# First stage of a two-layer decoder trunk on one core: rotary tables, bias tables, bias rows and the high part of h moved, and unit 0 put ahead of the values

## The chip, the cores and the metric

The kernel runs on one core of a Trainium2 chip. The metric is the device time of one execution in microseconds, the median of the timed runs.

## The reference

Two layers (DEPTH 2) work on 256 tokens of width 1024 in float32. Each layer modulates its input, projects it to three groups of attention heads, maps their output back, normalises, and does the same around an MLP. Only the first layer's beginning is touched by the change:

```python
mod = jax.nn.silu(c) @ ada_w[l] + ada_b[l]
sh_a, sc_a, g_a, sh_m, sc_m, g_m = [m_[:, None, :] for m_ in jnp.split(mod, 6, axis=-1)]
h = x * (1 + sc_a) + sh_a
parts = jnp.split(h @ w_in[l], SPLIT_POINTS, axis=-1)
...
ob, _ = banded_attention(rope(bq, positions), rope(bk, positions), bv, B_WINDOW - 1, sinks=sinks[l])
oc = nsa_attention(cq, ckc, cvc, cks, cvs, ckw, cvw, cg, cmp_pos[l], cmp_w1[l], cmp_w2[l], bias_c)
```

`rope` rotates the B heads by angles positions x frequencies; the A and C heads add a relative bias `rel_bias[t5_bucket(distance)]` to their scores.

## The kernel before, in words

**Split products.** A float32 product is made of three products of parts: `parts` (lines 174 to 183) writes the high part of a tile as fp32r with ScalarE (line 181, `whi`) and the low part with VectorE (line 182, `wlo`, the tile less its high part). `hT[:, 0]` and `hT[:, 1]` are the high and the low part of h, transposed.

**The first stage** (lines 898 to 938) goes over the 8 chunks of 128 columns of h, `kc`. For each chunk `first_h` (line 296) loads the chunk's modulation weights (1024 KB, line 139, `raw`) and, for every second chunk, x (line 302); multiplies the weights with silu(c) in 32 small matmuls (`gemv_mm`, line 169) into a PSUM bank `gv`; copies the result to `rs` (ScalarE, line 308); transposes x into columns 256 to 511 of the same bank (line 311); and brings scale and shift of the chunk into columns 128 and 129 of it (line 312). Then VectorE makes `md` (lines 314, 316) and `h32` (line 318), ScalarE the high part of hT (line 319) and VectorE the low part (line 320). `first_load` (line 323) loads the chunk's projection weights in two tiles `w0` (line 329; four buffers, so two chunks), and `first_chunk` (line 333) multiplies them with hT into seven open PSUM tiles (lines 341 to 344 for five pairs `prs`, lines 386 to 388 for two value tiles `vs`). An iteration of the loop traces gemv and loads of chunk kc, then the products of chunk kc-1, with the bank products and hT of chunk kc between them.

**Who sets the order.** The program is written tile by tile; when it is built, a scheduler lays the instructions of each engine into one queue, by the order in which they were traced and by when it estimates their inputs to be there, and puts in the semaphores. Each engine then works through its queue in that order. SyncE (SP) issues nearly all DMAs. `tc.issue_after(ins)` ties the instructions of its block that run on the engine of `ins` behind `ins` in that queue, and binds no other engine.

**START.** The string at place kc of `START` (line 34) says what else is traced after iteration kc: `r` loads a one-hot table and rel_bias, multiplies them (line 601, `bt`), copies the product (line 604) and sends it to DRAM through the POOL queue (`bias_rows`, line 592); each `b` loads a third of the `bias` table from there (`bias_tables`, line 612; 512 KB each); `p` loads `p2` (340 KB; sinks, compression positions and others), `c` loads `co` (373.5 KB; masks, rotary frequencies and others), and `o` makes the rotary tables `cosT` and `sinT` (`rope_tables`, line 621): a load of the positions, 14 VectorE instructions and two Sin on ScalarE, which need a table load. In the kernel before, `r` stands at chunk 0, `bpbco` at chunk 6 and a last `b` at chunk 7.

**After the stage** the open tiles are copied out (lines 995 to 1002, `vc_out` at line 948, whose Exp for the gates needs the Exp table), and the string `ORDER[0]` (line 32) is worked off: `k` projects and rotates the keys of the B heads (`bk_out`, line 970), `v` projects values (`vab_out`, line 965), `0` to `7` are the attention units of the C heads (`c_unit`, line 686: scores at line 697, `softmax_head` at lines 651 and 653), `s` is a step of the compression, and a dot is a step of the gemvs that fill in.

Of the kernel before, what the change touches and what calls it, by code (L numbers as in the profile page):

```python
# [13 lines left out]
AF = mybir.ActivationFunctionType  # L14
OP = mybir.AluOpType
# [13 lines left out]
EARLY = 3  # L29
FO = (1, 3)  # L30
TURN = 6
ORDER = ('kv0..21s4.3sa5.s.Acb.6.B7C..Ee', '.ts..q0412...ss3s.kva5cb.67AB.E..Ce')
GV = ('v', None, 'v', 'v', 'v')
START = ('r', '', '', '', '', '', 'bpbco', 'b', '')
GROUPS = ((0, 4, 0), (4, 8, 32))


# [84 lines left out]
def trunk_kernel(ctx: ExitStack, tc: tile.TileContext, a):  # L122
    nc = tc.nc
# [11 lines left out]
    p1 = cst.tile([128, NP1], F32, name="p1")  # L135
# [9 lines left out]
    co = cst.tile([128, NCO], F32, name="co")  # L145
# [3 lines left out]
    p2 = cst.tile([128, NP2], F32, name="p2")  # L149
# [7 lines left out]
    nc.vector.reciprocal(se[:, 1], se[:, 0])  # L157
    nc.vector.tensor_tensor(se[:, 2], cT, se[:, 1], op=OP.mult)
    silu = se[:, 2]
    crep = cst.tile([128, KC, 32], F32, name="crep")  # L160
    nc.vector.tensor_copy(crep, se[:, 2][:, :, None].to_broadcast([128, KC, 32]))

    hT = big.tile([128, 2, KC, S], F32R, name="hT")
# [132 lines left out]
    def first_h(kc):  # L296

        gv = ps.tile([128, 512], F32, name="gv", tag="pt")
        tp = gv[:, 256:512].rearrange("p (b t) -> p b t", b=2)
        t = rawload(a["ada0"][kc])  # L300
        if kc % 2 == 0:
            nc.sync.dma_start(x[:, :, kc * 128:kc * 128 + 256], a["x"][:, :, kc * 128:kc * 128 + 256])
        for k in range(KC):
            for s in range(2):
                j = 2 * (k % 2) + s
                end = gemv_mm(gv, t, k, j, (k * 2 + s) * 128, 128, k < 2, k >= KC - 2)
        rs = u2("rs")
        nc.scalar.activation(rs[:, :128], gv[:, :128], AF.Copy)
        yield end.ins
        for b in range(2):  # L310
            nc.tensor.transpose(tp[:, b], x[:, b, kc * 128:kc * 128 + 128], ident)
        nc.tensor.matmul(gv[:, 128:130], rs[:, :128], p1[:, 24:26], start=True, stop=True)
        md = sm.tile([128, 2], F32, name="md0")
        nc.vector.scalar_tensor_tensor(md[:, 0:1], gv[:, 128:129], 1.0, p1[:, 8 + 2 * kc:9 + 2 * kc],
                                       op0=OP.add, op1=OP.add)
        nc.vector.tensor_tensor(md[:, 1:2], gv[:, 129:130], p1[:, 9 + 2 * kc:10 + 2 * kc], op=OP.add)
        h32 = u2("h32")[:, :S]
        nc.vector.tensor_scalar(h32, gv[:, 256:512], md[:, 0:1], md[:, 1:2], op0=OP.mult, op1=OP.add)
        nc.scalar.activation(hT[:, 0, kc], h32, AF.Copy)
        nc.vector.tensor_tensor(hT[:, 1, kc], h32, hT[:, 0, kc].bitcast(F32), op=OP.subtract)  # L320
        yield

    def first_load(kc):
        off, _, n = CHUNK_OFF[0][f"k{kc}"]
        src = flat(a["w_in"][0], off, n)
        out = []
        for c, m in ((0, 768), (768, n - 768)):
            t = att.tile([128, 1024], F32, name="w0", tag="mx", bufs=4)
            nc.sync.dma_start(t[:, :m], src[:, c:c + m])
            out.append((t[:, :m], m))  # L330
        return out

    def first_chunk(kc, ts, prs, vs):

# [253 lines left out]
    bias = cst.tile([128, 12, 256], F32, name="bias")  # L588
    cosT = cst.tile([128, S], F32, name="cosT")
    sinT = cst.tile([128, S], F32, name="sinT")  # L590
# [30 lines left out]
    def rope_tables():  # L621
        pi32 = att.tile([128, S], I32, name="pi32", tag="pTc", bufs=2)
        src = a["positions"]
        nc.sync.dma_start(pi32, bass.AP(tensor=src.tensor, offset=src.offset, ap=[[0, 128], [1, S]]))
        t = new_P()
        an, k, f = t[:, 0], t[:, 1], t[:, 2]
# [17 lines left out]
        nc.vector.tensor_scalar(k, an, -1.0, -math.pi, op0=OP.mult, op1=OP.add)  # L644
        nc.vector.tensor_tensor(f, f, k, op=OP.max)
        nc.scalar.activation(sinT, f, AF.Sin)
        nc.vector.tensor_scalar(sinT, sinT, cc("sgn", 1), None, op0=OP.mult)


# [23 lines left out]
    def new_P():  # L673
        return att.tile([128, 4, S], F32, name="P", tag="P", bufs=4)
# [228 lines left out]
    btab = iter(())  # L903
    for kc in range(KC + 1):
        h = first_h(kc) if kc < KC else iter(())
        if kc == 0:
            next(h)
            w0 = first_load(0)
        if kc:
            ch = first_chunk(kc - 1, w0, prs, vs)  # L910
            end = next(h, None)
            if kc < KC:
                w0 = first_load(kc)
            for _ in range(FO[1]):
                next(ch)
            if FO[0] and end:
                with tc.issue_after(end):
                    next(ch)
            next(h, None)
            next(h, None)  # L920
            for _ in ch:
                pass
        else:
            next(h)
        for j in START[kc]:
            if j == "c":
                nc.sync.dma_start(co, a["co"])
            elif j == "r":
                btab = bias_tables(bias_rows())
            elif j == "p":  # L930
                nc.sync.dma_start(p2, a["p2"])
            elif j == "o":
                rope_tables()
            else:
                next(btab)
    for l in range(DEPTH):
        nc.vector.tensor_scalar(nsink[l], pp("sink", 4 * l, 4), -1.0, None, op0=OP.mult)
    fill += [gemv(0, 3, GV[0]), gemv(0, 2, GV[1])]
# [1 line left out]
    for l in range(DEPTH):  # L940
# [111 lines left out]
        jobs["+"] = lambda: next(btab)  # L1052
        for j in ORDER[l]:
            jobs[j]()
# [180 lines left out]
```

## Time and profile before

| | us |
|---|---|
| median of 3 runs | 701.38 (701.24 to 701.81) |
| the profiled execution | 700.93 |
| its span | 699.2 |

| engine | busy us | share of the span |
|---|---|---|
| TensorE (PE) | 672.6 | 96% |
| VectorE (DVE) | 490.3 | 70% |
| ScalarE (ACT) | 401.7 | 57% |
| GpSimd (POOL) | 41.0 | 6% |

The span runs from the first to the last instruction of the profiled execution; the rest of its time lies around it. An engine is idle when its next instruction waits; the profile names what ended such a wait. A matmul's duration overlaps the next one's, so the starts of a row of matmuls tell more than their durations.

### The profile page before, as it was taken

How to read it: one execution, taken by the hardware profiler on the slowest of the kernel's cores; microseconds unless marked ns; L12 is line 12 of the kernel's file. 1: busy time of each engine (PE TensorE's matmuls, PEld its weight loads, DVE VectorE, ACT ScalarE, POOL GpSimd, SP SyncE). 2: the span in 40 equal slices, each digit the busy share in tenths (PEclk: the TensorE clock that was granted, in tenths of full speed). 3: DMA queues.
4: the chain of work that ended last, by engine and by line, in shares of the span. 5: the costliest groups of instructions: out<-in, count | busy, mean ns of one | idle time of the engine just before them, and what ended most of it. 6: DMA issues, size and time to landing. Idle time of an engine off the chain costs nothing.

```text
span 699.2 us, 11153 instructions
## 1 busy us (share of the span) xinstructions
PE 672.6 (96%) x4284; PEld 549.5 (79%) x4284; DVE 490.3 (70%) x955; ACT 401.7 (57%) x791; POOL 41.0 (6%) x41
## 2 busy tenths in 40 slices
PE   5998899999999999999999999999999999999994
PEld 4898658458888888788889967867898888888883
DVE  3455865557798878888887866657679755555745
ACT  2346473776664656465746356688474655656641
POOL 0000100000400000000013020000130000000004
PEclk9999999999999999999999999999999999999998
DMA  8998586557369899899863858710448965555501
GB/s 323 354 356 329 211 331 213 187 218 321 137 229 373 296 389 322 322 345 340 302 240 121 328 187 281 266 60 2 181 129 305 372 214 193 208 183 182 181 0 61
DMA packets 29698, 167.68 MB, mean 240 GB/s; under 512 B 3215, under 2 KB 6827, under 8 KB 12108
## 3 DMA queue, kind: packets, MB, share of 16 engines
q1 hardware_dynamic: 29580, 166.94, 65.1%
q8 instruction: 34, 0.56, 0.3%
q14 instruction: 20, 0.16, 0.1%
q0 software_dynamic: 64, 0.02, 0.0%
HBM read 165.87 MB, written 1.08 MB: 239 GB/s over the span
## 4 chain that ended last, share of the span: by engine, by line
PE 88%; DVE 4%; ACT 3%; DMA 2%; issue 1%; SPq 0%; POOL 0%; POOLq 0%; DVEq 0%; ACTq 0%
PE mm L378 14%; PE mmv L395 8%; PE m L1129 8%; PE m L1130 8%; PE m L1131 8%; PE mm L379 7%; PE gv L169 3%; PE s L697 2%; PE mm L365 2%; PE wo L1066 2%; PE mm L367 2%; PE wo L1068 2%; PE tp L665 2%; PE wo L1067 2%; PE mm L366 2%; PE mm L341 2%
## 5 line engine op out<-in xcount | busy, mean ns | idle before, releaser
L182 DVE TENSOR_TENSOR wlo<-raw,whi 128x1024 fp32r<-128x1024 f32 (+3 forms) x174 | 196.6, 1154 | 49.7 <-ACT whi L181 48.1
L181 ACT ACTIVATE whi<-raw 128x1024 fp32r<-128x1024 f32 (+3 forms) x183 | 178.5, 1002 | 32.8 <-PE mm L378 14.5
L378 PE MATMUL mm<-hT,whi 128*128 128x512 f32 x416 | 148.0, 398 | 0.0
L379 PE MATMUL mm<-hT,wlo 128*128 128x256 f32 x416 | 116.2, 281 | 1.2 <-DVE wlo L182 1.2
L1129 PE MATMUL m<-whi,mx 128*128 128x512 f32 x256 | 100.0, 391 | 0.0
L1130 PE MATMUL m<-wlo,mx 128*128 128x512 f32 x256 | 100.0, 391 | 0.0
L1131 PE MATMUL m<-whi,mx 128*128 128x512 f32 x256 | 99.6, 390 | 0.0
L378 PEld LDWEIGHTS mm<-hT,whi 128*128 128x128 f32 x416 | 78.1, 188 | 20.7 <-issue 2.5
L379 PEld LDWEIGHTS mm<-hT,wlo 128*128 128x128 f32 x416 | 78.5, 189 | 3.4 <-DVE wlo L182 2.3
L244 DVE SCALAR_TENSOR_TENSOR qk<-raw,se,qk 128x1024 f32<-128x1024 f32 x56 | 71.2, 1282 | 0.6 <-DMA raw<-in_adag_dram 0.4
L381 ACT ACTIVATE P<-mm 128x256 f32<-128x256 f32 x52 | 19.7, 379 | 67.3 <-PE mm L379 67.2
L1129 PEld LDWEIGHTS m<-whi,mx 128*128 128x128 f32 x256 | 48.1, 188 | 10.2
L1131 PEld LDWEIGHTS m<-whi,mx 128*128 128x128 f32 x256 | 48.1, 188 | 10.1
L1130 PEld LDWEIGHTS m<-wlo,mx 128*128 128x128 f32 x256 | 48.1, 188 | 9.2
L395 PE MATMUL mmv<-whi,hT 128*128 128x256 f32 (+2 forms) x352 | 54.5, 299 | 0.0
L653 ACT ACTIVATE P<-P,sxt 128x128 f32<-128x128 f32 (+1 forms) x96 | 42.6, 446 | 17.2 <-DVE sxt L651 17.0
L395 PEld LDWEIGHTS mmv<-whi,hT 128*128 128x128 f32 x352 | 48.0, 190 | 1.4 <-issue 0.5
L365 PE MATMUL mm<-hT,whi 128*128 128x256 f32 x128 | 37.4, 292 | 0.0
L367 PE MATMUL mm<-hT,wlo 128*128 128x256 f32 x128 | 37.0, 289 | 0.0
L366 PE MATMUL mm<-hT,whi 128*128 128x256 f32 x128 | 36.8, 287 | 0.0
L430 POOL TENSOR_TENSOR ve<-ve,co 128x1 f32<-128x1 f32 x8 | 4.4, 552 | 548.1 <-DVE ve L429 443.6
L651 DVE CUSTOM_DVE_ANT_0 P<-s,bias 128x128 f32<-128x128 f32 (+1 forms) x80 | 25.7, 351 | 14.1 <-PE s L697 11.7
(219 smaller groups left out, 1102.2 us busy)
## 6 DMA issues: line engine op xcount, KB each, us to landing
raw<-in_mlp_w_dram SPq DMA_DIRECT2D x64, 1024.0 KB, 6.2
raw<-in_ada_dram SPq DMA_DIRECT2D x32, 1024.0 KB, 6.2
raw<-in_adag_dram SPq DMA_DIRECT2D x16, 1024.0 KB, 8.7
raw<-in_w_in_dram SPq DMA_DIRECT2D x9, 1024.0 KB, 7.0
raw<-in_cmp_w_dram SPq DMA_DIRECT2D x8, 1024.0 KB, 7.2
raw<-in_w_out_dram SPq DMA_DIRECT2D x8, 1024.0 KB, 6.4
w<-in_w_in_dram SPq DMA_DIRECT2D x8, 396.0 KB, 7.4
w<-in_w_in_dram SPq DMA_DIRECT2D x8, 384.0 KB, 6.3
```

Source lines behind the costliest of these rows:

```text
L181: nc.scalar.activation(hi, t, AF.Copy)
L182: (eng or nc.vector).tensor_tensor(lo, t, hi.bitcast(F32), op=OP.subtract)
L244: nc.vector.scalar_tensor_tensor(ac, src, by, ac, op0=OP.mult, op1=OP.add)
L365: nc.tensor.matmul(o[:, i], hi[:, c], hT[:, 0, kc], start=kc == 0, stop=False, skip_group_check=True)
L366: nc.tensor.matmul(o[:, i], hi[:, c], hT[:, 1, kc], start=False, stop=False, skip_group_check=True)
L367: nc.tensor.matmul(o[:, i], lo[:, c], hT[:, 0, kc], start=False, stop=kc == KC - 1, skip_group_check=True)
L378: nc.tensor.matmul(o, hi[:, c], hT[:, :, kc], start=kc == 0, stop=False, skip_group_check=True)
L379: nc.tensor.matmul(o[:, 0], lo[:, c], hT[:, 0, kc], start=False, stop=kc == KC - 1, skip_group_check=True)
L395: nc.tensor.matmul(o, hT[:, x_, kc, t], ws[kc][w_], start=kc == 0 and x_ + w_ == 0, stop=kc == KC - 1 and w_ == 1)
L1129: nc.tensor.matmul(o, f[:, 0, i, t], hi, start=first, stop=False)
L1130: nc.tensor.matmul(o, f[:, 0, i, t], lo, start=False, stop=False)
L1131: nc.tensor.matmul(o, f[:, 1, i, t], hi, start=False, stop=lastk)
```

## The change

- `START` becomes `('', 'r', 'c', '', 'o', '', '', '', 'bbpb')`: the bias rows are traced after iteration 1, `co` is loaded after iteration 2, the rotary tables are made after iteration 4, and the three bias loads and p2 come after iteration 8, behind all chunks. `first_load` returns its last DMA, and all of these loads but those of `r` are tied behind the last projection load that was traced.
- 1 is added once to the scales' constants in p1, so that md is one VectorE instruction.
- hT's high part is written by ScalarE straight from the bank, with md as scale and bias; h32 and the low part follow as before.
- After the second Sin a one-column Exp is run on ScalarE.
- In `ORDER[0]`, unit 0 stands ahead of the values.

```diff
-ORDER = ('kv0..21s4.3sa5.s.Acb.6.B7C..Ee', '.ts..q0412...ss3s.kva5cb.67AB.E..Ce')
+ORDER = ('k0v..21s4.3sa5.s.Acb.6.B7C..Ee', '.ts..q0412...ss3s.kva5cb.67AB.E..Ce')
-START = ('r', '', '', '', '', '', 'bpbco', 'b', '')
+START = ('', 'r', 'c', '', 'o', '', '', '', 'bbpb')
...
+    nc.vector.tensor_scalar(p1[:, 8:24:2], p1[:, 8:24:2], 1.0, None, op0=OP.add)
...
-        nc.vector.scalar_tensor_tensor(md[:, 0:1], gv[:, 128:129], 1.0, p1[:, 8 + 2 * kc:9 + 2 * kc],
-                                       op0=OP.add, op1=OP.add)
-        nc.vector.tensor_tensor(md[:, 1:2], gv[:, 129:130], p1[:, 9 + 2 * kc:10 + 2 * kc], op=OP.add)
+        nc.vector.tensor_tensor(md, gv[:, 128:130], p1[:, 8 + 2 * kc:10 + 2 * kc], op=OP.add)
+
+        nc.scalar.activation(hT[:, 0, kc], gv[:, 256:512], AF.Identity, bias=md[:, 1:2], scale=md[:, 0:1])
         h32 = u2("h32")[:, :S]
         nc.vector.tensor_scalar(h32, gv[:, 256:512], md[:, 0:1], md[:, 1:2], op0=OP.mult, op1=OP.add)
-        nc.scalar.activation(hT[:, 0, kc], h32, AF.Copy)
         nc.vector.tensor_tensor(hT[:, 1, kc], h32, hT[:, 0, kc].bitcast(F32), op=OP.subtract)
...
-            nc.sync.dma_start(t[:, :m], src[:, c:c + m])
             out.append((t[:, :m], m))
-        return out
+            last = nc.sync.dma_start(t[:, :m], src[:, c:c + m])
+        return out, last.ins
...
         nc.scalar.activation(sinT, f, AF.Sin)
+
+        nc.scalar.activation(k[:, 0:1], sinT[:, 0:1], AF.Exp)
         nc.vector.tensor_scalar(sinT, sinT, cc("sgn", 1), None, op0=OP.mult)
...
         for j in START[kc]:
-            if j == "c":
-                nc.sync.dma_start(co, a["co"])
-            elif j == "r":
+            if j == "r":
                 btab = bias_tables(bias_rows())
-            elif j == "p":
-                nc.sync.dma_start(p2, a["p2"])
-            elif j == "o":
-                rope_tables()
-            else:
-                next(btab)
+                continue
+
+            with tc.issue_after(loaded):
+                if j == "c":
+                    nc.sync.dma_start(co, a["co"])
+                elif j == "p":
+                    nc.sync.dma_start(p2, a["p2"])
+                elif j == "o":
+                    rope_tables()
+                else:
+                    next(btab)
```

## Rows read from the trace of the kernel before

**Rows 1.** The page: engines, busy us, share of the span, instructions.

```profile
PE 672.6 (96%) x4284; PEld 549.5 (79%) x4284; DVE 490.3 (70%) x955; ACT 401.7 (57%) x791; POOL 41.0 (6%) x41
```

**Rows 2.** Stretches: busy us (instructions) of each engine, granted clock, DMA share, GB/s.

```profile
core 0: us, PE busy (x) PEld busy (x) DVE busy (x) ACT busy (x) POOL busy (x), PEclk, DMA share, GB/s
...
45.00:50.00 5.00, 5.00 (x66) 4.67 (x65) 2.42 (x4) 2.18 (x4) 0.00 (x0) 1.00 1.04 386
...
60.00:65.00 5.00, 4.86 (x28) 4.66 (x28) 2.83 (x4) 2.60 (x5) 0.00 (x0) 0.66 0.50 167
...
75.00:80.00 5.00, 2.95 (x15) 2.31 (x14) 5.00 (x13) 1.58 (x7) 0.00 (x0) 1.00 0.61 203
```

**Rows 3.** TensorE's waits, 0 to 110 us: total, times, longest us.

```profile
PE mm L341 <- ACT hT L319: 2.7, 4, 1.6
PE sw L883 <- ACT ct L878: 1.8, 1, 1.8
PE gv L311 <- ACT rs L308: 1.4, 1, 1.4
```

**Rows 4.** Timeline, chunk 0: start, us, engine, line, instruction, [idle before <-releaser].

```profile
9.71 0.69 PE L311 MATMUL gv<-p,x 128*128 128x128 f32 x2 [1.37 <-ACT rs L308]
...
10.73 0.16 DVE L314 SCALAR_TENSOR_TENSOR md<-gv,p 128x1 f32<-128x1 f32 x1 [0.25 <-PE gv L312]
...
10.94 1.57 PE L601 MATMUL bt<-P,rb 33*32 33x384 f32 x4 [0.33 <-DMA rb<-in_rel_bias_dram]
...
11.56 0.42 ACT L319 ACTIVATE hT<-h 128x256 fp32r<-128x256 f32 x1 [0.65 <-DVE h L318]
...
12.43 0.79 PE L341 MATMUL mm<-hT,whi 128*128 128x256 f32 x2
```

**Rows 5.** Timeline, chunk 1.

```profile
20.83 0.74 PE L341 MATMUL mm<-hT,whi 128*128 128x256 f32 x4 [0.60 <-ACT hT L319]
21.13 0.42 DVE L320 TENSOR_TENSOR hT<-h,hT 128x256 fp32r<-128x256 f32 x1
...
21.79 0.28 PE L343 MATMUL mm<-hT,whi 128*128 128x256 f32 x1
```

**Rows 6.** Timeline, chunk 7: first TensorE, then VectorE.

```profile
57.83 0.28 PE L312 MATMUL gv<-p,rs 128*128 128x2 f32 x2
59.73 1.55 PE L341 MATMUL mm<-hT,whi 128*128 128x256 f32 x5 [1.62 <-ACT hT L319]
...
58.21 0.16 DVE L314 SCALAR_TENSOR_TENSOR md<-gv,p 128x1 f32<-128x1 f32 x1 [1.14 <-PE gv L312]
...
58.35 0.41 DVE L645 TENSOR_TENSOR P<-P 128x256 f32<-128x256 f32 x1
```

**Rows 7.** Timeline, SyncE's queue from 38 us on (start, us of issue).

```profile
38.74 0.43 SPq L616 DMA_DIRECT2D bias<-bd  x1
...
41.48 0.68 SPq L139 DMA_DIRECT2D raw<-in_ada_dram  x1
```

**Rows 8.** Timeline, ScalarE: the table load for Exp and the Exp behind it.

```profile
66.58 1.28 ACT L950 ACT_TABLE_LOAD   x1
67.88 0.19 ACT L950 ACTIVATE ge<-mmv 128x24 f32<-128x24 f32 x1
```

**Rows 9.** Timeline, VectorE and ScalarE from 70 to 79 us.

```profile
70.22 0.29 DVE L651 CUSTOM_DVE_ANT_0 P<-s,bias 128x128 f32<-128x128 f32 x1 [0.59 <-PE s L697]
...
75.03 2.68 DVE L182 TENSOR_TENSOR wlo<-raw,whi 128x768 fp32r<-128x768 f32 x3
...
78.73 0.36 ACT L878 ACTIVATE ct<-mm 128x256 f32<-128x256 f32 x1
```

**Rows 10.** Timeline, VectorE: first and last of the 14 rotary instructions.

```profile
52.27 0.29 DVE L627 CAST P<-pi 128x256 f32<-128x256 int32 x1
...
59.25 0.35 DVE L647 TENSOR_SCALAR sinT<-sinT,co 128x256 f32<-128x256 f32 x1
```

**Rows 11.** Groups by line, ScalarE: busy us, mean ns of one, idle before.

```profile
L471 ACT ACTIVATE tp<-tp,sb 128x128 f32<-128x128 f32 x24 | 10.3, 431 | 2.2 <-PE tp L464 1.6
L436 ACT ACTIVATE P<-wo,ve 128x512 f32<-128x512 f32 x4 | 3.1, 778 | 0.1
```

More of the change, by code (lines that the diff above doesn't have):

```diff
@@ L907, in trunk_kernel @@
             next(h)
-            w0 = first_load(0)
+            w0, _ = first_load(0)
         if kc:
@@ L912, in trunk_kernel @@
             if kc < KC:
-                w0 = first_load(kc)
+                w0, loaded = first_load(kc)
             for _ in range(FO[1]):
```

## The prediction

> **What bounds the kernel now.** I read the page first: TensorE is busy for 96% of the span [rows 1], so time is only to be had where it idles or runs at its lower clock. The list of TensorE's waits up to 110 us comes second: the first products of a chunk wait four times for hT, 2.7 us in all, a rotary product waits 1.8 us once, and the transposes of x wait 1.4 us once [rows 3]. Third, the table of stretches: from 45 to 50 us TensorE is busy for all 5 us, so in mid-stage it and not the loads sets the pace; in 60 to 65 us its mean granted clock is 0.66, and in 75 to 80 us it is busy for 2.95 us of 5 [rows 2]. So the change can act in four places: the first chunk, the gaps ahead of chunks 1 to 3, the tail at chunk 7, and the start of the attention units. After 80 us TensorE is the bound again, so what is gained or lost before it moves the end by the same amount. The profiled execution took 700.93 us, span 699.2; the sum is made against it, and the median, 701.38, lies 0.45 above.
>
> **The changes part by part.**
>
> *h's high part from the bank.* Now the chain is md, a second md, h32, then hT's high part on ScalarE. In chunk 0 it runs from 10.73 us to the end of hT at 11.56 + 0.42 = 11.98 us, 1.25 us [rows 4]. Afterwards it is one md and one ScalarE Identity that reads the bank with scale and bias. No 256-column form of it is in the trace; Identity of that kind takes 0.43 us at 128 columns and 0.78 us at 512 [rows 11], which puts 256 columns at 0.55 us by a straight line between them (bounds 0.43 and 0.78). md 0.16, a handover of 0.05, and 0.55 make 0.76 us: the high part comes 0.49 us sooner (0.26 to 0.61). The low part doesn't: h32 follows the ScalarE read, and then the subtraction. I take the reads as one after the other for a reason in the trace: the transposes of x write other columns of the bank than those which rs is copied from, need nothing of rs, and yet waited 1.37 us for that copy [rows 4]. So accesses of one bank by two engines are kept apart here. The Trainium skill says the same of two readers (PSUM — Partial Sum Buffer, section on bank collisions: ScalarE and VectorE must not read one bank at the same time, and software has to order them); side by side instead, the low part too would come about 0.5 us sooner, and the sum below would be some 0.6 us better.
> What it is worth: the gaps ahead of chunks 1, 2 and 3 are 2.7 less the tail's 1.62 [rows 3, 6], that is 1.1 us. At chunk 1 the gap is 0.60 us, but the low part ends at 21.13 + 0.42 = 21.55 us as before [rows 5], and the seven products that need only the high part last 0.96 us, from 20.83 to the next one's start at 21.79 [rows 5], so there I count 0.2 of 0.6, and the two smaller gaps nearly whole: **+0.6** (0 to 1.1). In chunk 0 the first products could start at about 11.5 rather than 12.43 us [rows 4], and then run into the low part: **+0.3** (-0.2 to 0.9).
>
> *Bias rows behind chunk 0.* Three loads leave SyncE's queue ahead of chunk 1's, which come out sooner. But the one-hot product, 1.57 us at the lower clock, lay in the time in which chunk 0 waited for hT [rows 4]; in the next iteration it meets a nearly full TensorE and takes a bank in turn with the next gv. At the higher clock I take half, 0.79 us, less a little that falls into what is left of chunk 1's gap: **-0.7** (-1.57 to 0).
>
> *Biases and p2 behind the last chunk.* SyncE issues bias, p2, bias, co and positions from 38.74 us on, and only then, at 41.48, the last chunk's modulation weights [rows 7]. The order written for TensorE answers to that: gemv 7 stands behind nearly all of chunk 6, so that after the bank product of chunk 7 (57.83 us) nothing is left to do, and TensorE idles 1.62 us until hT is there [rows 6]. With bias and p2 behind chunk 7's loads, its weights leave some 2 us sooner, and gemv 7 can stand as early as the other chunks' do, with a dozen products of chunk 6 behind it. If so the gap is covered: +1.62. If not, it still loses 0.49 us and the rotary instruction that stood in front of h32 (0.41 us at 58.35, of which some 0.3 delayed it) [rows 6]: about +0.8. I take **+1.4**. The clock: what came before its fall was this gap, and the granted 0.66 over 5 us [rows 2] is 3.4 us at 1.2 GHz, during which 1.7 us of work at 2.4 GHz was lost. With the gap gone I take **+1.7** (0 to 1.7; the longer wait of 1.8 us at 79 us did not lower it in its own stretch [rows 2, 3], so a small gap need not either).
> The late tables have cover: unit 0 first uses bias at 70.22 us [rows 9], about 25 us after they are issued, and nothing that reads p2 is on TensorE's path before that. The three loads of weights that stand behind them in the queue find the same bytes ahead of them as before. If that cover were gone, unit 0 would wait for a transfer of 512 KB, 1.4 us at 386 GB/s [rows 2].
>
> *Rotary tables in mid-stage.* 14 VectorE instructions of some 0.3 to 0.4 us each, 5.0 us in sum, from the cast at 52.27 to the sign at 59.25 us [rows 10], two of ScalarE and two table loads of 1.28 us [rows 8] move into chunks 4 to 6. There VectorE is busy 2.42 and ScalarE 2.18 of 5 us [rows 2], so there is room; but both work in order, and a md, h32 or hT that stands behind such a piece is late by its length. hT has the 0.49 us just won to give. Co (373.5 KB, 1.0 us at the rate above) and positions now go ahead of chunks 3 and 5; a chunk is loaded two ahead. I take **-0.3** (-3.3 to 0, the lower end with three quarters of the VectorE work in one piece ahead of one hT less 0.5).
>
> *Table of Exp.* The load at 66.58 us, in the middle of a full ScalarE [rows 8], goes; a one-column Exp pulls it into mid-stage. *Unit 0 ahead of values.* TensorE waits 1.82 us at 79.15 us [rows 3] for ScalarE's copy of K (78.73 us), which stands behind unit 0's exponentials, which wait for VectorE's three low parts of the values (75.03 us, 2.68 us) [rows 9]. Unit 0's minima ahead of these let the exponentials and the copy run sooner; the price is that the values' low parts come later by the same minima, about 1.3 us for two more heads and unit 0's reciprocal and scalings, five pieces of no more than a head's 0.29 us each [rows 9]. Against the 1.28 + 1.82 us that can go I count **+0.8** (-1.3 to 2.0). The skill would make this load dearer (ScalarE: Activation LUTs, What ACT_TABLE_LOAD costs: 1283 ns and a drain of about 1380 ns); by that up to 1.4 us more would go, while the trace has the next Exp 1.30 us after the load began [rows 8], so the drain isn't in this number.
>
> The addition of 1 to p1 (one small VectorE instruction) lies in the start, where everything waits for the first weights: 0.
>
> **Sum:** 0.6 + 0.3 - 0.7 + 1.4 + 1.7 - 0.3 + 0.8 = 3.8 us. 700.93 - 3.8 = 697.1 for a profiled execution, 697.6 against the median.
>
> **The rivals.**
> *All gaps close.* Tail covered, the product of the bias rows in a gap, and nothing left of the wait at 79 us: 1.1 + 0.5 - 0.1 + 1.62 + 1.7 + 2.0 = 6.8 us, 694.6. For it: all these waits name work that the change moves. Against: VectorE was busy without a break in 75 to 80 us [rows 2], and the same work is still to be done there.
> *The tail keeps its gap.* gemv 7 stays behind chunk 6, only the chain is shorter, and the clock falls all the same: 0.6 + 0.3 - 0.7 + 0.8 + 0 - 0.3 + 0.8 = 1.5 us, 699.9. For it: the order of TensorE's queue follows estimated landings, and I have not seen the new one.
> *Unit 0 takes the values' time.* The low parts of the values become what TensorE waits for, -1.3 instead of +0.8: 1.7 us are left, 699.7. It would also be so if the edit does nothing: unit 0's first products already stand ahead of the values'.
> *Slower: rotary work ahead of hT.* The rotary chain stands as one piece in front of one chunk's h32. Price: 5.0 us of VectorE with a ScalarE table load and Sin between (1.28 + 0.42), less 0.5 slack and some 1 us of products left, is a TensorE gap of 5.2 us and then 1.7 us for the clock; 3.8 + 0.3 - 6.9 = -2.8, or 704.2. It is slower than before as soon as the gap, with the clock, is over 4.1 us. Against it: in the kernel before, the same instructions were laid between those of chunk 7, and only one of them came ahead of h32 [rows 6].
>
> **How the numbers follow.** Forecast 0.50; all gaps close 0.15; the tail keeps its gap 0.20; unit 0 takes the values' time 0.06; slower 0.09. The predicted time is the forecast's, 697.6. The range goes from 694.0 (all gaps close, and the start near its upper bound) to 701.2, which takes in the tail's rival with 1.3 us of mid-stage loss; what is left out is the slower case and a little at each end. About 0.2%, 1.4 us, is what a measurement of this kernel can tell from no change: faster, below 699.98, are the forecast, the best case and half of the two near 699.8, in all 0.78; within, 0.14; slower, 0.08.
>
> **What would show it.** Right: SyncE issues chunk 7's weights before any bias; gemv 7 starts within a few products of chunk 6's begin; no gap over 0.5 us ahead of chunk 7; no stretch of lower clock about 60 us; no table load after 60 us; K's copy ahead of the values' low parts. Wrong: a gap over 1 us in 30 to 55 us with VectorE or ScalarE on rotary work as its releaser; a low clock there; products that wait for hT's low part; a longer idle stretch between 70 and 85 us.

## The result, and the profile of the changed kernel

The changed kernel takes **707.25 us** (median of 4 runs, 706.74 to 707.48) against 701.44 for the kernel before beside it: a ratio of **1.0083, 95% interval 1.0071 to 1.0095**. It is 5.8 us slower; the forecast was 3.8 us faster. The profiled execution has a span of 705.7 us, 6.5 more than before.

Four marks on TensorE's timeline cut that difference into stages: the transposes of x of chunks 2 and 6, the last product of the first stage ("end of the stage"), and the first product of the output projection. The last column adds up the prediction's terms by these stages.

| stage | before, us | changed, us | gain | predicted |
|---|---|---|---|---|
| start to the transposes of chunk 2 | 25.5 | 25.1 | +0.4 | -0.2 |
| chunk 2 to chunk 6 | 24.6 | 28.2 | -3.6 | +0.1 |
| chunk 6 to the end of the stage | 15.9 | 11.8 | +4.1 | +3.1 |
| end of the stage to the output projection | 90.0 | 97.7 | **-7.7** | +0.8 |
| from there to the end of the span | 543.1 | 542.9 | +0.2 | 0 |

A mark can move without a gain or a loss, when TensorE does other work ahead of it; the sums up to the end of the stage and behind it are safer. Up to the end of the stage 0.9 us are won (3.0 predicted), behind it 7.7 are lost (+0.8 predicted).

TensorE's busy time rose by 4.7 us [rows 1], though its work is the same:

```profile
PE 677.3 (96%) x4284; PEld 551.0 (78%) x4284; DVE 490.1 (69%) x948; ACT 403.2 (57%) x792; POOL 41.7 (6%) x41
```

The table of stretches says where (busy us and instructions of PE, PEld, DVE, ACT, POOL; granted clock; DMA share; GB/s; as [rows 2]):

```profile
45.00:50.00 5.00, 4.08 (x43) 3.84 (x45) 3.88 (x9) 3.46 (x6) 0.15 (x1) 1.00 0.67 235
60.00:65.00 5.00, 5.00 (x44) 5.00 (x42) 1.12 (x4) 2.28 (x4) 0.00 (x0) 1.00 1.01 423
...
70.00:75.00 5.00, 2.13 (x11) 1.59 (x10) 4.92 (x12) 2.04 (x4) 0.10 (x1) 0.90 0.17 26
75.00:80.00 5.00, 5.00 (x30) 4.90 (x30) 3.92 (x8) 1.73 (x5) 0.00 (x0) 0.76 0.91 367
...
90.00:95.00 5.00, 3.97 (x39) 2.05 (x32) 3.88 (x11) 1.93 (x10) 0.00 (x0) 0.95 0.68 239
95.00:100.00 5.00, 5.00 (x15) 1.70 (x15) 1.51 (x10) 3.13 (x12) 0.00 (x0) 0.50 0.93 357
100.00:105.00 5.00, 5.00 (x31) 2.80 (x34) 1.30 (x9) 2.27 (x8) 0.00 (x0) 0.53 0.29 69
```

At 60 us the clock no longer falls and TensorE is full: the tail came out as hoped. In 45 to 50 us TensorE now idles 0.9 us, where it was full. From 70 to 75 us it is busy for 2.13 us only; about then its clock falls to 1.2 GHz for 3.4 us (5 us times 0.10 and 0.24, each over a half), and again for 10.2 us in 90 to 105 us. An estimate from these rows: 13.6 us at half the clock, with TensorE busy nearly all of it, cost 6.8 us. In the kernel before, the clock was full in those stretches:

```profile
95.00:100.00 5.00, 5.00 (x61) 2.90 (x62) 1.61 (x11) 3.99 (x16) 0.00 (x0) 1.00 0.97 374
```

TensorE's waits from 0 to 110 us (engine, line, releaser: us in total, times, longest us; as [rows 3], without the 6.3 us for the first weights at the start):

```profile
PE mm L368 <- DVE wlo L184: 2.6, 1, 2.6
PE mm L342 <- ACT hT L318: 2.4, 3, 0.9
...
PE hid L838 <- ACT cpt L835: 1.0, 1, 1.0
...
```

The longest of these is new: a product of the keys waits 2.63 us for the low part of its weights. Why is told by the timelines of the two kernels. Changed (start, us, engine, line, instruction, idle before):

```profile
59.91 0.56 ACT L318 ACTIVATE hT<-gv,md 128x256 fp32r<-128x256 f32 x1 [2.18 <-DVE md L316]
63.10 0.60 ACT L1001 ACTIVATE KK<-mm 128x512 f32<-128x512 f32 x1 [2.62 <-PE mm L345]
...
66.67 1.10 ACT L183 ACTIVATE whi<-raw 128x1024 fp32r<-128x1024 f32 x1
...
73.70 0.39 PE L368 MATMUL mm<-hT,wlo 128*128 128x256 f32 x1 [2.63 <-DVE wlo L184]
...
72.44 1.21 DVE L184 TENSOR_TENSOR wlo<-raw,whi 128x1024 fp32r<-128x1024 f32 x1
```

Before:

```profile
60.34 1.04 ACT L181 ACTIVATE whi<-raw 128x1024 fp32r<-128x1024 f32 x1
63.68 0.60 ACT L995 ACTIVATE KK<-mm 128x512 f32<-128x512 f32 x1 [2.31 <-PE mm L344]
...
61.62 1.22 DVE L182 TENSOR_TENSOR wlo<-raw,whi 128x1024 fp32r<-128x1024 f32 x1
```

The tile of 128x1024 is the keys' weights (`t10`). Before, ScalarE splits it ahead of the copy of K, in idle time, and the 24 products of the keys fill TensorE from 66.0 to 69.4 us. In the changed kernel it stands behind nine copies, at 66.67 us. That part ends at 67.77 us, but its low part stands behind the rotations of the heads (lines 887 to 892) and four pieces of line 822 in VectorE's queue, and starts at 72.44 us only. The data wasn't what it waited for. SyncE issues the load at 51.56 us, and it lands 8.9 us later, at 60.5 us, just as ScalarE goes idle for 2.62 us. First the queue, then the load's row (KB, us from issue to landing), each with the row of the kernel before last:

```profile
46.01 3.39 SPq L331 DMA_DIRECT2D w<-in_w_in_dram  x2
49.45 0.97 SPq L617 DMA_DIRECT2D bias<-bd  x2
50.48 0.50 SPq L937 DMA_DIRECT2D p<-in_p_dram  x1
51.08 0.38 SPq L617 DMA_DIRECT2D bias<-bd  x1
51.56 1.63 SPq L139 DMA_DIRECT2D raw<-in_w_in_dram  x3
...
47.30 2.66 SPq L139 DMA_DIRECT2D raw<-in_w_in_dram  x3
```

```profile
raw<-in_w_in_dram SPq DMA_DIRECT2D x1, 512.0 KB, 8.9
...
raw<-in_w_in_dram SPq DMA_DIRECT2D x1, 512.0 KB, 9.7
```

So the order of ScalarE's and VectorE's queues is at fault, which is fixed when the program is built. That the load was expected late there, behind the biases and p2, and that the split was laid behind the copies for this reason, is a reading; the run that moves the load (below) bears it out. In mid-stage more rows bear on the rotary work: VectorE about 40 us, the product that waits behind it, and the products of chunk 5 with md and hT ahead of them.

```profile
40.12 0.28 DVE L628 CAST P<-pi 128x256 f32<-128x256 int32 x1
40.31 0.98 DVE L184 TENSOR_TENSOR wlo<-w,whi 128x792 fp32r<-128x792 f32 x1
41.21 0.54 DVE L320 TENSOR_SCALAR h<-gv,md 128x256 f32<-128x256 f32 x1
41.66 0.34 DVE L629 TENSOR_SCALAR P<-P,co 128x256 f32<-128x256 f32 x1
41.92 0.42 DVE L321 TENSOR_TENSOR hT<-h,hT 128x256 fp32r<-128x256 f32 x1
...
42.39 0.38 PE L344 MATMUL mm<-hT,whi 128*128 128x256 f32 x1 [0.29 <-DVE hT L321]
...
47.66 0.16 DVE L316 TENSOR_TENSOR md<-gv,p 128x2 f32<-128x2 f32 x1 [1.02 <-PE gv L314]
...
47.86 0.57 ACT L318 ACTIVATE hT<-gv,md 128x256 fp32r<-128x256 f32 x1 [1.37 <-DVE md L316]
...
48.48 0.74 PE L342 MATMUL mm<-hT,whi 128*128 128x256 f32 x4 [0.92 <-ACT hT L318]
```

Two rotary pieces stand ahead of the low part of hT, and a product waits 0.29 us for it. The wait of 0.92 us is of another kind: VectorE and ScalarE had been idle, md and hT follow each other at once, and TensorE had nothing else to do meanwhile. And chunk 1, as [rows 5]:

```profile
18.95 0.56 ACT L318 ACTIVATE hT<-gv,md 128x256 fp32r<-128x256 f32 x1 [1.82 <-DVE md L316]
...
19.55 0.54 DVE L320 TENSOR_SCALAR h<-gv,md 128x256 f32<-128x256 f32 x1 [0.64 <-ACT hT L318]
...
20.50 0.84 PE L602 MATMUL bt<-P,rb 33*32 33x384 f32 x4
```

The read of the bank costs 0.56 us (estimated 0.55), h32 waits for it, the gap ahead of chunk 1 (0.60 us) is gone, and the one-hot product lies between products of chunk 0, with 0.77 us to the next start.

### The profile page after: what moved, and what is told of

Its sections match the earlier page's. It is cut to its first block, busy times and chain, and to the rows that moved or that the text cites. A ratio compares the mean times of both kernels' runs of the same rounds, so it can differ in the third digit from the quotient of the medians.

```text
span 705.7 us, 11150 instructions
## 1 busy us (share of the span) xinstructions
PE 677.3 (96%) x4284; PEld 551.0 (78%) x4284; DVE 490.1 (69%) x948; ACT 403.2 (57%) x792; POOL 41.7 (6%) x41
## 3 DMA queue, kind: packets, MB, share of 16 engines
q1 hardware_dynamic: 29580, 166.94, 64.5%
## 4 chain that ended last, share of the span: by engine, by line
PE 91%; DVE 4%; ACT 3%; DMA 1%; issue 1%; SPq 0%; POOL 0%; POOLq 0%; DVEq 0%; ACTq 0%
PE mm L379 14%; PE mmv L396 9%; PE m L1135 8%; PE m L1136 8%; PE m L1137 8%; PE mm L380 7%; PE s L700 3%; PE gv L171 3%; PE tp L668 3%; PE mm L368 2%; PE mm L366 2%; PE mm L367 2%; PE wo L1072 2%; PE wo L1074 2%; PE wo L1073 2%; PE acc L716 2%
## 5 line engine op out<-in xcount | busy, mean ns | idle before, releaser
L654 DVE CUSTOM_DVE_ANT_0 P<-s,bias 128x128 f32<-128x128 f32 (+1 forms) x80 | 25.8, 352 | 22.2 <-PE s L700 19.8
```

## The experiments

**The theory:** the keys' weights, split late because their load stands behind biases and p2, let TensorE run dry, and the clock falls after that. **Its rivals:** unit 0 ahead of the values does it, as its softmax steps and the values' split stand in each other's way; or the rotary work in mid-stage does. Ratios are against the kernel before on the same chip (its medians are 701.1 to 701.2 us); marks and clock are of the profiled execution. "Slower" in the text goes by the ratio, which takes in all executions and lies off the ratio of the medians where they spread; "less than the changed kernel" goes by the medians (707.25). In the kernels that have a part undone, and in those with the rows, the biases or the rotary tables alone, the loads of `START` but those of `r` are tied behind the projection loads, as in the changed kernel.

| | median us | ratio, 95% interval | end of the stage | output projection | us at 1.2 GHz behind the stage |
|---|---|---|---|---|---|
| before | 701.1 | 1 | 66.0 | 156.1 | 0 (3.4 in the tail) |
| changed, again | 706.93 | 1.0086 (1.0072 to 1.0099) | 64.5 | 162.0 | 13.6 |
| biases undone | 703.32 | 1.0034 (1.0022 to 1.0046) | 66.0 | 158.8 | 6.8 |
| unit 0 undone | 703.10 | 1.0023 (1.0009 to 1.0038) | 65.3 | 158.3 | 3.4 |
| both undone | 700.88 | 0.9999 (0.9990 to 1.0009) | 65.9 | 155.8 | 0 |
| rotary undone | 700.56 | 0.9995 (0.9986 to 1.0005) | 65.0 | 157.1 | 3.4 |
| bank alone | 702.28 | 1.0012 (1.0002 to 1.0021) | 66.5 | 156.9 | 0 (3.4 in the tail) |
| biases alone | 702.17 | 1.0022 (1.0003 to 1.0041) | 63.7 | 158.2 | 10.2 |
| unit 0 alone | 702.21 | 1.0021 (1.0004 to 1.0038) | 66.7 | 161.3 | 10.2 (3.4 in the tail) |
| rotary alone | 702.40 | 1.0017 (1.0007 to 1.0026) | 66.3 | 158.0 | 3.4 |
| rows alone | 700.76 | 1.0000 (0.9989 to 1.0011) | 67.2 | 158.9 | 3.4 (3.4 in the tail) |
| keys' weights first | 701.44 | 1.0006 (0.9997 to 1.0015) | 64.9 | 156.8 | 6.8 |
| + values first, rotary at 6 | 701.79 | 1.0008 (0.9999 to 1.0017) | 65.5 | 157.4 | 3.4 |
| values first, rotary at 6 | 701.03 | 0.9999 (0.9990 to 1.0007) | 65.8 | 156.6 | 0 |
| before + biases, keys first | 700.25 | 0.9988 (0.9980 to 0.9997) | 64.5 | 156.1 | 3.4 |
| + Exp | 700.41 | 0.9996 (0.9986 to 1.0007) | 64.3 | 155.0 | 3.4 |
| + bank | 701.71 | 1.0000 (0.9989 to 1.0012) | 65.4 | 156.4 | 3.4 |

**Parts undone in the changed kernel.** First the biases back in place:

```diff
-START = ('', 'r', 'c', '', 'o', '', '', '', 'bbpb')
+START = ('', 'r', 'c', '', 'o', '', 'bpb', 'b', '')
```

> The changed kernel with START ('', 'r', 'c', '', 'o', '', 'bpb', 'b', ''): biases and p2 at chunks 6 and 7 again, all else as changed. Theory A (the loads of biases and p2, now ahead of the weights of the B heads' keys, push the split of these weights behind all copies of the stage's tiles; TensorE runs dry and its clock falls after the stage): the split stands ahead of K's copy again, the 2.6 us wait for its low part at 73.7 us and both low-clock stretches after the stage go; 700.5 to 702.5 us. Rival B (unit 0 ahead of the values is what empties TensorE): as changed, 706 to 708. Rival C (the rotary tables in mid-stage cost it): as changed, 706 to 708.

Measured: 703.32 us, 3.9 less than the changed kernel, above the theory's range and below the rivals'. The wait for the keys' low part is gone, and the gap of the tail is back (0.92 us). Waits of 1.56 us for unit 0's softmax and 1.02 us for the values' high part stand behind the stage instead, and 6.8 us of lower clock. Then unit 0 behind the values:

```diff
-ORDER = ('k0v..21s4.3sa5.s.Acb.6.B7C..Ee', ...
+ORDER = ('kv0..21s4.3sa5.s.Acb.6.B7C..Ee', ...
```

> The changed kernel with the values ahead of unit 0 again in ORDER. Theory A: the keys' weights are still split late, so the empty stretch and the low clock stay; 705.5 to 708 us. Rival B: both go, 700 to 702.5. Rival C: 706 to 708.

Measured: 703.10 us, 4.1 less: outside all three ranges. The wait for the keys' low part is the same as in the changed kernel, so it doesn't come from unit 0's place:

```profile
PE mm L368 <- DVE wlo L184: 2.6, 1, 2.6
```

But only 3.4 us of lower clock follow, not 13.6. Both edits together:

> The changed kernel with biases and p2 at chunks 6 and 7 and with the values ahead of unit 0. Theory A: within 1 us of the run with only the biases back. Rival B: within 1 us of the run with only the order back, and far below the run with only the biases back. Rival C: 705 to 708, since the rotary tables stay in mid-stage.

Measured: 700.88 us, the time of the kernel before, and 2.2 to 2.4 us below the runs with one of the two undone, which none of the three had forecast. Without the two steps nothing is lost, with the rotary work still in mid-stage, and what is left of the change gains nothing. Last, the rotary tables and co at iteration 6:

```diff
-START = ('', 'r', 'c', '', 'o', '', '', '', 'bbpb')
+START = ('', 'r', '', '', '', '', 'co', '', 'bbpb')
```

> The changed kernel with co and the rotary tables at chunk 6 again (behind its projection loads), biases and p2 still last. Theory A: mid-stage gives back what it lost between chunks 2 and 6 (about 3 us by the starts of the gemvs), but the keys' weights stay late; 703 to 706 us. Rival C: 699 to 701.5. Rival B: 706 to 708.

Measured: 700.56 us, 6.7 less, in the range of the rival that blames the rotary work. But mid-stage isn't where they come from. Chunk 2 to chunk 6 takes 26.1 instead of 28.2 us, chunk 6 to the end of the stage 13.9 instead of 11.8, and the stage ends at 65.0 us, as in the changed kernel (65.1, and 64.5 in its second profile). The two profiles differ by 5.6 us (spans of 700.1 and 705.7), and all of it comes from behind the stage: the split of the keys' weights stands there 1.7 us earlier (64.97 us) and its low part 6 us earlier (66.39), TensorE's waits are other ones, and the clock falls for 3.4 us instead of 13.6. So the parts aren't added; each shifts the queues behind the stage, and the clock magnifies it.

**Parts alone in the kernel before.** The bank (with the 1 added to p1, as in the diff of the change):

```diff
+        nc.scalar.activation(hT[:, 0, kc], gv[:, 256:512], AF.Identity, bias=md[:, 1:2], scale=md[:, 0:1])
         nc.vector.tensor_scalar(h32, gv[:, 256:512], md[:, 0:1], md[:, 1:2], op0=OP.mult, op1=OP.add)
-        nc.scalar.activation(hT[:, 0, kc], h32, AF.Copy)
```

> The kernel before with hT's high part straight from the bank and the 1 added to p1, nothing else. Theory (shorter chain only): the three waits for hT ahead of chunks 1 to 3 (1.1 us together) shrink to 0.3 to 0.6 us and chunk 7's from 1.62 to about 1.1 us; the stage ends 0.8 to 2.5 us sooner, the more if the clock doesn't fall; 698.5 to 700.5 us. Rival (this edit is what made the way from chunk 2 to chunk 3 longer by 1.4 us, by low parts that now wait for ScalarE's read of the bank): that way is 7.5 us or longer, 700.5 to 702.5 us.

Measured: 702.28 us, 0.8 slower. The gaps ahead of chunks 1 to 3 do go (from chunk 1 to chunk 6 30.5 instead of 31.2 us), but chunk 1's transposes come 1.1 us later. The time is the rival's, its sign isn't: chunk 2 to chunk 3 takes 6.4 us, not 7.5. TensorE's timeline of chunk 0:

```profile
11.29 0.79 PE L340 MATMUL mm<-hT,whi 128*128 128x256 f32 x2 [0.92 <-ACT hT L316]
...
12.48 1.49 PE L600 MATMUL bt<-P,rb 33*32 33x384 f32 x4
```

The first products start 1.1 us sooner than in [rows 4], but the one-hot product, which lay in the wait for hT, now stands between them with 1.43 us. Products also stay long for longer: one of 256 columns still takes 0.41 us at 16.46 us, as at 1.2 GHz (75.17 us in the changed kernel), where before one of 280 columns takes 0.29 us from 16.02 us on. (The granted clock of the rows reads 1.00 there.) That the one-hot product puts this off isn't shown, for it differs as much between profiles with the same beginning, here the first of "+ Exp", the second of "before + biases, keys first":

```profile
14.93 0.29 PE L387 MATMUL mmv<-whi,hT 128*128 128x280 f32 x1
...
16.15 0.43 PE L389 MATMUL mmv<-whi,hT 128*128 128x280 f32 x1
```

So whether this part needs the move of the rows is open.

Biases alone, and unit 0 alone:

```diff
-START = ('r', '', '', '', '', '', 'bpbco', 'b', '')
+START = ('r', '', '', '', '', '', 'co', '', 'bbpb')
```

> The kernel before with biases and p2 behind all chunks, co and the rotary tables at chunk 6, bias rows at chunk 0, values ahead of unit 0. If the late split of the keys' weights is enough to empty TensorE after the stage: its low part ends a wait of 2 us or more between 70 and 75 us, the clock falls there (3.4 us or more), and the way from the stage's end to the output projection is 2.5 us longer or more than 90.0; 700 to 703 us with 2 to 4 us won in the tail. If it needs unit 0 ahead of the values too: that way is within 1 us of 90.0, and the time is 697 to 699.

Measured: 702.17 us, 1.5 slower. The stage ends 2.3 us sooner, and the way behind it is 4.5 us longer, again with a wait for the keys' low part; the clock falls even ahead of it, at 67 us, behind a wait of 0.69 us for unit 0's softmax:

```profile
74.90 0.39 PE L368 MATMUL mm<-hT,wlo 128*128 128x256 f32 x1 [1.41 <-DVE wlo L183]
```

```diff
-ORDER = ('kv0..21s4.3sa5.s.Acb.6.B7C..Ee', ...
+ORDER = ('k0v..21s4.3sa5.s.Acb.6.B7C..Ee', ...
```

> The kernel before with unit 0 ahead of the values, nothing else. If this order alone empties TensorE: waits of 2 us or more and a low clock between 70 and 100 us, 702.5 to 705 us. If it does harm only where the keys' weights come late as well: 700 to 702, and the way from the stage's end to the output projection within 1 us of 90.0.

Measured: 702.21 us, 1.5 slower, between the two ranges. TensorE waits for unit 0's softmax and for the values' high part instead of K's copy, 2.1 us in place of 1.8 [rows 3]:

```profile
76.31 0.67 PE L697 MATMUL s<-KK,qk 64*128 64x256 f32 x2 [1.41 <-DVE sxt L651]
77.65 2.66 PE L395 MATMUL mmv<-whi,hT 128*128 128x384 f32 x9 [0.68 <-ACT whi L181]
```

In both kernels two of ten executions took about 706 us. They have a mean granted clock of 0.985; those near 701 have 0.992 to 0.996. The profile of unit 0 alone is of such an execution, and has 10.2 us of lower clock behind the stage. So the same program keeps or loses several us, and the mean clock goes with it.

Rotary tables alone:

```diff
-START = ('r', '', '', '', '', '', 'bpbco', 'b', '')
+START = ('r', '', 'c', '', 'o', '', 'bpb', 'b', '')
```

> The kernel before with co behind chunk 2 and the rotary tables behind chunk 4, no Exp behind the second Sin. If the rotary work delays hT in mid-stage: the way from chunk 2's bank product to chunk 6's is 26 to 28 us instead of 24.6, with waits for hT at chunks 4 and 5; chunk 7 gains up to 0.5 us; 702 to 704.5 us. If mid-stage has room for it: 24.6 to 25.2 us, and 700.5 to 701.5.

Measured: 702.40 us, 1.2 slower. Chunk 2 to chunk 6 takes 27.1 us, 2.5 more, with waits of 2.5 us in all there (0.5 before), among them one for which the profile names no releaser:

```profile
34.07 0.74 PE L342 MATMUL mm<-hT,whi 128*128 128x256 f32 x4 [0.69 <-ACT hT L320]
...
48.10 1.08 PE L170 MATMUL gv<-raw,crep 128*32 128x128 f32 x32 [1.22 <-issue]
```

But chunk 6 to the end of the stage takes 13.9 instead of 15.9 us, without a fall of the clock, so that the stage ends 0.3 us later only. Behind it the way to the output projection is 1.7 us longer, with 3.4 us of lower clock.

And the bias rows alone:

```diff
-START = ('r', '', '', '', '', '', 'bpbco', 'b', '')
+START = ('', 'r', '', '', '', '', 'bpbco', 'b', '')
```

> The kernel before; only the bias rows are traced after iteration 1 instead of 0. Theory (the one-hot product is cheap where chunk 0 waits for hT, and costs its full length at the higher clock in the next iteration): 0.8 us more, 701.5 to 702.5. Rival (the new order of chunks 2 and 3 in the changed kernel, where the interval between the transposes of x was 7.3 to 7.9 us instead of 6.5, comes from the rows' move): over 702.5, with that interval over 7 us.

Measured: 700.76 us, no difference. The interval from chunk 2's transposes to chunk 3's is 7.2 us instead of 6.5, as the rival has it, and chunk 2 to chunk 6 takes 26.3 instead of 24.6 us, but the median shows no loss. (The profile is of an execution of 703.66 us.) Here too the time follows the clock: seven of the twelve executions with a mean clock of 0.995 or more took 699.8 to 700.9 us, three with 0.993 took 701.4 to 702.6, two with 0.991 took 703.7. A stretch of 3.4 us at half the clock is 0.0024 of the mean over 700 us, and costs 1.7 us, by the same estimate as above.

**The keys' weights by themselves.** The changed kernel once more, as the yardstick:

> The changed kernel, once more, as the yardstick for the three kernels beside it. If its loss is a fixed amount of waiting, its runs lie together near 707.2. If the larger part is falls of the clock that are not the same in each execution, they spread over 702 to 707.5, as those of the kernels with the biases alone and with unit 0 alone did (702.2, with two of ten near 706).

Measured: 706.93 us (706.28 to 708.02, 4 runs), with the two stretches of lower clock at the same places. The mean clock is 0.985 to 0.989 in all eight executions of this kernel, so most or all of this comes every time. Then their load ahead of the biases, with its buffer taken there, nothing else:

```diff
-START = ('', 'r', 'c', '', 'o', '', '', '', 'bbpb')
+START = ('', 'r', 'c', '', 'o', '', '', '', 'tbbpb')
...
+            if j == "t":
+                off, nk, n = CHUNK_OFF[0]["t10"]
+                early_k = raw.tile([128, 2048], F32, name="raw", tag="raw")
+                loaded = nc.sync.dma_start(early_k[:, :nk * n], flat(a["w_in"][0], off, nk * n)).ins
+                continue
...
-            B["k"] = rope(t_pair(wchunk(l, "t10"), 1), 1, 1.0)[:, 0]
+            w = split(early_k, 8, 128) if l == 0 else wchunk(l, "t10")
+            B["k"] = rope(t_pair(w, 1), 1, 1.0)[:, 0]
```

> The changed kernel; only the load of the keys' weights is put ahead of the biases and p2, behind the last chunk. Theory (the keys' weights are split late because their load stands behind 1.5 MB of biases and p2): the wait of 2.63 us for their low part at 73.7 us goes, and unit 0 follows sooner. Without the fall of the clock that came behind it, 702 to 704; with unit 0's place as the only thing left, 702.2 as for that edit alone, and 1.4 for the mid-stage. Rival (unit 0 ahead of the values keeps TensorE thin by itself): the split comes early, yet the clock falls behind the stage all the same, 705 to 707.

Measured: 701.44 us, **5.5 less than the changed kernel** in its second run, and below the theory's range, by moving one load of 512 KB some 2 us up the queue (49.13 instead of 51.56 us). The split now stands where ScalarE had idled, and the keys' products fill TensorE behind the stage:

```profile
57.30 1.05 ACT L183 ACTIVATE whi<-raw 128x1024 fp32r<-128x1024 f32 x1
...
72.92 1.12 PE L700 MATMUL s<-KK,qk 64*128 64x256 f32 x4 [1.42 <-DVE sxt L654]
75.03 1.01 PE L396 MATMUL mmv<-whi,hT 128*128 128x384 f32 x2 [0.99 <-ACT whi L183]
```

```profile
95.00:100.00 5.00, 5.00 (x52) 2.53 (x50) 2.64 (x19) 4.84 (x19) 0.00 (x0) 1.00 0.95 380
```

The second fall, at 94 us, is gone; unit 0's waits remain, with 6.8 us of lower clock behind them. Of the theory, this shows that the place of this load decides over most of the loss in the changed kernel; the waits of unit 0 are real too. What is left:

```diff
-ORDER = ('k0v..21s4.3sa5.s.Acb.6.B7C..Ee', ...
-START = ('', 'r', 'c', '', 'o', '', '', '', 'tbbpb')
+ORDER = ('kv0..21s4.3sa5.s.Acb.6.B7C..Ee', ...
+START = ('', 'r', '', '', '', '', 'co', '', 'tbbpb')
```

> The changed kernel with the keys' weights ahead of the biases, the values ahead of unit 0 as in the kernel before, and co with the rotary tables behind iteration 6. Theory: each of the three steps that cost time is undone, and what is left are the gains of the tail (4.1 us over chunk 6 to the end of the stage), of the gaps at chunks 1 to 3 (0.7) and nothing lost behind the stage: 696.5 to 699.5. Rival (the gain of the tail is work moved past the end of the stage and comes back there): 700.5 to 702, as with both parts undone.

Measured: 701.79 us: the rival, not the theory. And the same without `t`:

> The kernel of the run before this one, but with the keys' weights behind the biases and p2 as in the changed kernel. Theory: the wait for their low part is there again, 1.4 to 2.6 us, and with the clock that may fall behind it the time is 2 to 5 us above the run before this one, 700 to 703. Rival (the place of the keys' weights does not matter): the two agree to within 0.7 us.

Measured: 701.03 us. With the values first and the rotary work late, the keys' weights behind the biases do no harm; the time is 0.8 us less instead of 2 to 5 more. Their split stands at 65.75 us here, 0.9 us sooner than in the changed kernel, its low part 5.3 us sooner, and no product waits for it:

```profile
67.17 1.22 DVE L184 TENSOR_TENSOR wlo<-raw,whi 128x1024 fp32r<-128x1024 f32 x1
```

So the place of the load in SyncE's queue isn't enough for the harm; it takes the place of the low part in VectorE's, which the other parts shift as well.

**Where the tail's gain goes.** The kernel before, with `START = ('r', '', '', '', '', '', 'co', '', 'tbbpb')` and the lines for `t` as above:

> The kernel before with biases and p2 behind the last chunk, and the keys' weights ahead of them; all else as before. The biases alone brought the end of the stage to 63.7 us (66.0 before) and lost 4.5 us behind it, with a wait of 1.4 us for the low part of the keys' weights. Theory (that late split is what turns the tail's gain into a loss): the end of the stage stays near 63.7, the wait goes, and the way from there to the output projection is again about 90 to 91 us: 699 to 700. Rival (what is won in the tail is waited for behind it whatever stands first, because VectorE and ScalarE have the same work to do there): 700.5 to 702.

Measured: 700.25 us, between the two, 0.12% below the kernel before (interval 0.03 to 0.20%): the best of all, and hardly more than can be told from no change. The stage ends 1.5 us sooner, and the output projection starts at the same time. TensorE's waits, then ScalarE and VectorE:

```profile
PE sw L885 <- ACT ct L880: 3.0, 1, 3.0
```

```profile
77.11 0.36 ACT L880 ACTIVATE ct<-mm 128x256 f32<-128x256 f32 x1
...
72.92 3.55 DVE L183 TENSOR_TENSOR wlo<-raw,whi 128x768 fp32r<-128x768 f32 x4
```

K's copy comes 1.6 us sooner than before (78.73 us, [rows 9]), behind VectorE's low parts and the exponentials, and the wait for it is 3.0 us instead of 1.82. The clock, which no longer falls in the tail, falls behind this wait, again for 3.4 us. So in this profile the gap and the fall of the tail weren't removed; they moved behind the stage. The last two add the Exp of one column, and then the bank:

```diff
         nc.scalar.activation(sinT, f, AF.Sin)
+        nc.scalar.activation(k[:, 0:1], sinT[:, 0:1], AF.Exp)
```

> The run before this one, and the Exp table loaded behind the second Sin. Theory: a table load of 1.28 us leaves a ScalarE that is full behind the stage, 0 to 1.3 us less than the run before this one. Rival (the copies that stand behind it wait for VectorE in any case): the same to 0.5 us.

> The run before this one, and h's high part from the bank. Theory: the gaps ahead of chunks 1 to 3 go, 0.7 us less, and the tail's gap is shorter, so 698 to 699.5, below the kernel before. Rival (the bank alone was 0.8 us slower than before, with a later rise of the clock in the first chunk): 0 to 1 us more than the run before this one.

Measured: 700.41 and 701.71 us. The table load that goes from the path behind the stage is worth nothing, as the rival has it; the bank, with the rows still at chunk 0, is 1.3 us up by the medians, but the two intervals overlap and the executions spread over 699.3 to 703.2 us, so that this isn't told from no change.

## Why the prediction was wrong

- **High part from the bank: right in its rows; its effect on the start isn't settled.** 0.56 us for the Identity (0.55 estimated), h32 behind it with a wait of 0.64 us, and the gap ahead of chunk 1 gone. The Trainium skill (PSUM — Partial Sum Buffer, the section on bank collisions) says that ScalarE and VectorE must not read one bank at once; the wait in the row of chunk 1 agrees. The start to chunk 2 gained 0.4 us where -0.2 was predicted, but profiles of kernels with the same beginning have this mark anywhere from 24.5 (changed again) to 25.8 us (rotary at 6).
- **Bias rows:** 0.77 us on the path, as estimated (0.79); alone, they changed nothing that can be measured in the median.
- **Biases last, the tail: right in its signs, but not by the biases alone** (+4.1 for +3.1). The gap ahead of chunk 7 and the lower clock at 60 us are gone, and gemv 7 starts 2.3 us behind the transposes of chunk 6, not 5.7. But chunk 7's weights don't leave 2 us sooner: they are issued at 41.74 us (41.48 before). With the biases undone the stretch still takes 13.0 us, with the rotary tables undone 13.9: 1.2 of the 4.1 us go with the biases, 2.1 with the rotary tables. Biases alone win 2.1.
- **The cover of the late tables: the step that failed.** The prediction said that the three loads of weights behind them "find the same bytes ahead of them as before", and so priced nothing. The bytes are the same, but the load is issued 4.3 us later (51.56 instead of 47.30 us) and lands 3.5 us later (60.5 instead of 57.0), while the stage ends 0.9 us sooner. What decided wasn't the transfer, which was there when ScalarE went idle. It was the place of the split in ScalarE's and VectorE's queues: a wait of 2.63 us on TensorE. With this load ahead of the biases again, 5.5 of the 5.8 us are back. The prediction itself says that the order of TensorE's queue follows estimated landings, and used it for gemv 7 alone.
- **Rotary tables: mis-sized in mid-stage, and not apart from the tail.** -0.3 was taken, of -3.3 to 0; alone they cost 2.5 us between chunks 2 and 6, and 2.1 us are won there when they are undone. But the tail gives back 2.0 us in the one kernel and takes 2.1 in the other, so that little is left at the end of the stage. Together, mid-stage and tail were forecast at +3.2 us, and measured +0.5. The mechanism named (pieces ahead of hT) shows as one wait of 0.29 us; that of 0.92 us has no piece ahead of hT.
- **What the -3.6 us of chunk 2 to chunk 6 are made of.** Rotary alone +2.5 us, rows alone +1.7, bank alone -0.6: in sum the 3.6. With the rows moved TensorE is mostly busy in the longer time, so that part of it is work that lay elsewhere before; the prediction had priced it nowhere between these marks.
- **Unit 0 ahead of the values: wrong in sign.** +0.8 was taken; alone it cost 1.5 us. The wait for K's copy went, but waits for unit 0's softmax and the values' high part came. The nearest rival (TensorE waits for the values' low parts) priced it at -1.3 and had a chance of 0.06.
- **The clock was priced once only, in the tail.** The prediction took the clock behind the stage as given ("After 80 us TensorE is the bound again"). There the larger loss is: by the estimate above 6.8 of 7.7 us, 5.1 of them behind 90 us. The rival that forecast slower had its gap in mid-stage; the gap came behind the stage, 2.63 us long.

Still open: in the kernel with values first and rotary at 6, no stretch of lower clock and only short waits are left, and yet it takes 701.0 us. Its gain from chunk 6 on (2.0 us) is nearly gone by the end of the stage, which comes at 65.8 us: chunk 2 to chunk 6 takes 26.1 us, 1.5 more than before, with waits of 0.4 us (0.5 before). Why TensorE is busy for longer there isn't shown; the kernel with the rows alone has it too. Why the changed kernel's clock falls about 94 us in both of its profiles, and that of most relatives not, isn't settled either: there the last wait before it is 1.03 us, and in 90 to 95 us TensorE is busy for 3.97 us, against 5.00 before. With unit 0 undone the wait of 2.64 us stays and this fall doesn't come, so the two aren't simply cause and effect.

## What to carry to other kernels

When loads are moved to the end of a queue, look for the load that now comes next behind them, and for the place of the work that uses it in the queues of the other engines: where their order is fixed by estimates, that work can go behind other work, though its data is there in time. Price a wait on TensorE twice, by its length and by the lower clock that may follow; a gap that is closed at one place and comes back at another has gained nothing. Parts of a change that all act on one crowded place don't add up: here four parts that cost 0.8 to 1.5 us alone, and a fifth that cost nothing, made 5.8 together, and undoing one of them alone gave 3.9 to 6.7 back.

## What the runs showed of the hardware that was not expected

- The clock fell behind idle times of 0.7 to 3 us, and executions of the same program differ (701 or 706 us, mean clock 0.992 to 0.996 or 0.985, for unit 0 alone and the biases alone). Behind the longest wait (3.0 us) came 3.4 us at 1.2 GHz, behind that of 1.03 us 10.2. Waits of one length differ too: behind the 1.82 us for K's copy it didn't fall in the kernel before, and fell for 3.4 us with the rotary tables alone.
- At the start, products get short (280 columns in 0.29 instead of 0.43 us) at a time that isn't the same in two profiles with one beginning: before 14.93 us in one, behind 16.15 us in the other, while the granted clock of the rows reads 1.00.
